# One layer of a streaming encoder on one core: gate writes on another queue, a later exponential, attention values on halves of the array's columns, other banks for the last tiles' branches

## The chip, the cores and the metric

The kernel runs on one core of a Trainium2 chip. The metric is device time in microseconds (us), the median over runs of the whole program. The engines are TensorE (PE, with its weight loads as PEld), VectorE (DVE), ScalarE (ACT), GpSimd (POOL) and SyncE (SP, which in this kernel only issues DMAs). ACT and SP each issue DMAs on a queue of their own, ACTq and SPq in the profile. The clock that TensorE is granted (PEclk) is given as a share of full speed.

## The reference, cut to what matters

One layer on 512 tokens of 1024 channels, all float32. The parts that the change touches are the attention's product with the values, the two branches' output projections, and the choice of 16 experts per head with its softmax.

```python
h = rms_norm(x, attn_norm_g)
q, k, v, qi, ki, wi, glu_in, gates = jnp.split(h @ w_in, _split_points(), axis=-1)
# DSA attention: top-k admissible keys by an indexer score, bias, softmax
probs = jax.nn.softmax(logits, axis=-1).astype(vg.dtype)
y_att = jnp.einsum('bqhk,bqkhd->bqhd', probs, vg) @ w_att_out      # 8 heads of 64
y_conv = conformer_conv(glu_in, conv_w, conv_b, conv_ln_g, conv_ln_b, w_conv_out)
g = jax.nn.sigmoid(gates + b_gate).reshape(B, S, N_BRANCH, D)
x = x + (g[:, :, 0, :] * y_att + g[:, :, 1, :] * y_conv) @ w_out
# PEER mixer on rms_norm(x): 8 heads, 2 x 128 keys, 16 of 256 candidates
sc = jnp.einsum('bshcd,hckd->bshck', q, sub_keys)
sv, si = lax.top_k(sc, PEER_TOPK)
cand_s = (sv[..., 0, :, None] + sv[..., 1, None, :]).reshape(B, S, PEER_HEADS, n_cand)
cand_i = (si[..., 0, :, None] * N_KEYS + si[..., 1, None, :]).reshape(...)
top_s, top_j = lax.top_k(cand_s, PEER_TOPK)
eidx = jnp.take_along_axis(cand_i, top_j, axis=-1)
gate = jax.nn.softmax(top_s.astype(jnp.float32), axis=-1)
act = jax.nn.gelu(jnp.einsum('tnd,td->tn', expert_u[eidx], h)) * gate
x = x + jnp.einsum('tn,tnd->td', act, expert_v[eidx])
# x += sigmoid(rms_norm(x) W_g) * (p W_p)
```

## The kernel before, in words

The 512 tokens are four tiles of 128. Tile 0 goes ahead of tiles 1 to 3. Its experts are gathered row by row (POOL's indirect DMAs, `grow`, with DVE's products `grow` and `acc`); tiles 1 to 3 (384 tokens, TD) go through all 16,384 experts densely, 128 experts at a time. The stages, by the span's clock:

- 0 to about 300 us: the projection `w_in`, the attention of tile 0 and the indexer.
- 300 to 408 us: branches, residual and query of tile 0, with the attention of tiles 1 to 3 mixed in. For each tile and each pair of heads, `softmax` makes the logits (L550), and `weigh` transposes the probabilities (L570, evicted at L572 into `PT`), multiplies `V` by them (L576) and evicts the result (L580). `V`'s 128 columns are those of two heads and `PT` holds the probabilities of both, so each product forms four 64x128 blocks, of which the two on the diagonal are used.
- 408 to 457 us: `branches` for tiles 1 to 3, with 128x384 products in four PSUM banks per half of the channels (`nat_T`, L141). L629 multiplies each by its gate. PSUM has three pools of banks: `mm`, `at` and `tp`.
- 457 to 592 us: residual, per-layer embedding and the query of the mixer.
- 592 to 955 us, the warm stage: 64 steps `u_step`, each of 24 products of 128x384 (L972 to L974) into a `tp` bank, evicted by ACT through Gelu (`sg`, L975). ACT and DVE split each block of expert weights, loaded by SP (`ut`, L961), into `uh` (L964) and `ul` (L965). Mixed into these steps is `gates_dense` for tiles 1, 2 and 3: `select` finds the 16 experts of each head and their gates (`ijg`, written by L711 and L736), PE transposes them (L910), DVE makes one-hot rows (L930 to L933), `scatter` multiplies them (L948, L949), ACT evicts into `stg` (L951), and four DMAs of 512 KB for every 32 tokens write `G_d` in DRAM (L956). There are 12 such bursts of four. `G_d` is read back from 955 us on (`gi`).
- 955 to 1700 us: the other 64 blocks of experts, and the products with `vt`. Then 75 us for what is left of the mixer and for the embedding.

The order of the instructions on each engine is found by a scheduler from the order of the program's text, the buffers and some priorities (`high_priority` for the loads and the split of `ut`); `work()` is advanced in steps between the `u_step`s. The order is fixed when the kernel is built. An engine runs its instructions in that order, and an issue on SP or ACT that has to wait holds up what stands behind it. ACT's Exp and its Gelu use different function tables; each change is an ACT_TABLE_LOAD of 1.28 us.

`select` is a generator in three pieces: the candidates, then the first `lookup` (which of the candidates, as sums over 16 masks on DVE), then the second.

Of the kernel before, what the change touches and what calls it, by code (L numbers as in the profile page):

```python
# [11 lines left out]
F32 = mybir.dt.float32  # L12
# [6 lines left out]
ALU = mybir.AluOpType  # L19
# [5 lines left out]
P = 128  # L25
# [43 lines left out]
def layer_kernel(ctx: ExitStack, tc: tile.TileContext, a, out):  # L69
# [7 lines left out]
    def mm(name="mm"):  # L77
        return psum.tile([P, 512], F32, name="mm", bufs=4)
# [4 lines left out]
    def tp():  # L83
        return psum.tile([P, 512], F32, name="tp", bufs=2)
# [28 lines left out]
    class Stream:  # L113
# [16 lines left out]
            if self.hook:  # L130
                self.hook(n)

        def nat_T(self, pieces, K, x):
            M = sum(p[2] for p in pieces) // P
            ps = [mm()[:, :x.shape[-1]] for _ in range(M)]
            for c0 in range(0, K, 2):
                raw, _ = self.load(pieces, c0)
                self.behind()
                for c in range(2):
                    for m in range(M):  # L140
                        pe.matmul(ps[m], raw[:, c, m * P:(m + 1) * P], x[:, c0 + c, :], start=(c0 + c == 0),  # L141
                                  stop=(c0 + c == K - 1))
            return ps
# [418 lines left out]
    def weigh(ap_, top, qt, pr_, L):  # L562
        nk = qt + 1
        PT = ap_.tile([P, top, 2, P], F32, name="PT", bufs=2)
        for k0 in range(0, nk, 2):
            n = min(2, nk - k0)
            p = tp()
            for kk in range(n):
                for s in range(2):
                    pe.transpose(p[:, (2 * kk + s) * P:(2 * kk + s + 1) * P],  # L570
                                 L[:, s, (k0 + kk) * P:(k0 + kk + 1) * P], ident)
            act.activation(PT[:, k0:k0 + n], p[:, :2 * n * P].rearrange("p (k s q) -> p k s q", k=n, s=2), AF.Copy)  # L572
        yield
        av = tp()[:, :2 * P]
        for kt in range(nk):
            pe.matmul(av, V[:, kt, pr_ * P:(pr_ + 1) * P], PT[:, kt].rearrange("p s q -> p (s q)"),  # L576
                      start=(kt == 0), stop=(kt == nk - 1))
        for s in range(2):
            sl = slice(64 * s, 64 * s + 64)
            act.activation(attT[sl, pr_, qt * P:(qt + 1) * P], av[sl, s * P:(s + 1) * P], AF.Copy)  # L580
        yield

    def attention(ap_, tiles):
# [35 lines left out]
    def branches(pl, q0, N, mixed, mlo=None, tick=None):  # L619
        mix = []  # L620
        for br, (w, x2) in enumerate(((a["w_att_out"], attT), (a["w_conv_out"], convT))):
            for n in range(2):
                ps = W.nat_T([(w, 512 * n, 512)], 4, x2[:, :, q0:q0 + N])
                for m in range(4):
                    c = 4 * n + m
                    g = pl.tile([P, N], F32, name="gld", bufs=4)
                    sp.dma_start(out=g, in_=gT_d[8 * br + c][:, q0:q0 + N])
                    y = pl.tile([P, N], F32, name=f"ymx{br}", bufs=8 - 6 * br)
                    v.scalar_tensor_tensor(y, g, 1.0, ps[m], op0=ALU.add, op1=ALU.mult)  # L629
                    if br == 0:  # L630
                        mix.append(y)
                    elif mlo is None:
                        v.tensor_add(mixed[:, c, :], y, mix[c])
                    else:
                        v.tensor_add(y, y, mix[c])
                        act.activation(mixed[:, c, :], y, AF.Copy)
                        v.tensor_sub(mlo[:, c, :], y, f(mixed[:, c, :]))
                if tick:
                    tick(BTICK)
# [64 lines left out]
    def select(t, gate, i_out, j_out):  # L704
# [17 lines left out]
        for h in range(H):  # L722
# [6 lines left out]
        yield  # L729
        ex = sl_.tile([P, H, 16], F32, name="ex", bufs=1)  # L730
        v.tensor_tensor(out=ex, in0=ts, in1=ts[:, :, 0:1].to_broadcast([P, H, 16]), op=ALU.subtract)
        act.activation(ex, ex, AF.Exp)
        sm = sl_.tile([P, H], F32, name="exs", bufs=1)
        v.tensor_reduce(out=sm, in_=ex, axis=AX, op=ALU.add)
        v.reciprocal(sm, sm)
        v.tensor_tensor(out=gate.rearrange("p (k h) -> p h k", h=H), in0=ex,  # L736
                        in1=sm.unsqueeze(2).to_broadcast([P, H, 16]), op=ALU.mult)
        w = sl_.tile([P, P], F16, name="wpos", bufs=1)
        v.tensor_copy(w.rearrange("p (k h) -> p k h", h=H), tj.rearrange("p h k -> p k h"))
        sT = sl_.tile([P, 2, 16, H], F16, name="sT", bufs=1)  # L740
        v.tensor_copy(sT.rearrange("p c k h -> p h c k"), si[:, t].rearrange("p (h c) k -> p h c k", c=2))
        dl = sl_.tile([P, 3, 16, H], F16, name="dl", bufs=1)
        v.tensor_copy(dl[:, 1], dstart)
        act.activation(dl[:, 0:3:2, 0], sT[:, :, 0], AF.Copy)
        v.tensor_sub(dl[:, 0:3:2, 1:16], sT[:, :, 1:16], sT[:, :, 0:15])
        mk = sl_.tile([P, 16, P], F16, name="mk", bufs=1)
        md = sl_.tile([P, 2, 16, P], F16, name="md", bufs=1)
# [9 lines left out]

        lookup(w, edges[:, 0], 0, 2)
        yield
        add(i_out, md[:, 0, 0], md[:, 0, 1])  # L760
        add(mk[:, 0], md[:, 1, 0], md[:, 1, 1])
        v.tensor_sub(w, w, mk[:, 0])
        lookup(w, edges[:, 1], 2, 1)
        add(j_out, md[:, 0, 0], md[:, 0, 1])
        yield

    def sel0():
# [174 lines left out]
    def scatter(tt, part, t0, q0, stg, ohj, og):  # L942
# [10 lines left out]
        if t0 + q0 == 12:  # L953
            c0 = tt * P + 32 * part
            for b0 in range(0, P // 4, 8):
                act.dma_start(out=G_d[b0:b0 + 8, :, c0:c0 + 32, :].rearrange("b j t f -> j b (t f)"),  # L956
                              in_=stg[:, b0:b0 + 8].rearrange("p b t f -> p b (t f)"))

    def u_prep(i):
# [277 lines left out]
```

## Time and profile before

| | us |
|---|---|
| median of 3 runs | 1781.04 |
| lowest and highest run | 1773.59, 1781.09 |
| the profiled run's own time | 1776.63 |
| span of the profiled run | 1774.9 |
| PE busy in it | 1717.2 (97%) |
| DVE busy | 1362.3 (77%) |
| ACT busy | 660.9 (37%) |

The span is the time from the first to the last instruction in the profile; 1.7 us of the run lie around it. The profiled run took 4.4 us less than the median. A busy share is a mean over the whole span, so a stage that waits is not to be seen in it; the rows further below are taken by stage.

### The profile page before, as it was taken

The numbers are of one execution on the slowest core, as the hardware profiler recorded it, in microseconds if no ns is written. First come the engines' busy times: TensorE is split into PE (matmuls) and PEld (weight loads), VectorE is DVE, ScalarE is ACT, GpSimd is POOL, SyncE is SP. The second block draws the span as 40 slices with busy tenths as digits, with TensorE's granted clock in tenths as the row PEclk, the third lists the DMA queues.
The fourth block names the chain that finished last, engine by engine and source line by source line (L and its number), as shares of the span: only waits on it lengthen the run. The fifth ranks groups of instructions, "written<-read, shape, count | busy, mean of one in ns | idle before, by whom it ended". The sixth has DMA issues, their size and how long they took to land.

```text
span 1774.9 us, 24360 instructions
## 1 busy us (share of the span) xinstructions
PE 1717.2 (97%) x9033; PEld 1487.6 (84%) x9033; DVE 1362.3 (77%) x2489; ACT 660.9 (37%) x981; POOL 427.5 (24%) x301
## 2 busy tenths in 40 slices
PE   6999999999999899999999999999999999999998
PEld 5777677586788888999999999999999988888887
DVE  4889779648769999996857878877877857667763
ACT  3233343340353244444444333333333333334431
POOL 0021000211112113120113645445545511111100
PEclk9999999999999999999999999999999999999999
DMA  5432325756875468788899999899989878888921
GB/s 163 145 120 84 100 84 184 255 174 192 293 266 155 129 227 280 236 273 260 288 293 378 391 329 337 321 340 330 353 306 344 308 260 311 311 291 314 376 87 69
DMA packets 189815, 441.74 MB, mean 249 GB/s; under 512 B 15192, under 2 KB 76888, under 8 KB 189440
## 3 DMA queue, kind: packets, MB, share of 16 engines
q1 hardware_dynamic: 100528, 273.72, 45.1%
q0 software_dynamic: 36864, 134.23, 21.4%
q10 hardware_dynamic: 52304, 32.24, 6.1%
q8 instruction: 71, 1.16, 0.3%
q14 instruction: 48, 0.39, 0.1%
HBM read 391.86 MB, written 52.46 MB: 250 GB/s over the span
## 4 chain that ended last, share of the span: by engine, by line
PE 59%; DVE 7%; issue 4%; DMA 2%; ACT 1%; POOL 0%; SPq 0%; DVEq 0%; ACTq 0%; POOLq 0%
PE tp L972 9%; PE tp L973 9%; PE tp L974 9%; PE mm L1059 6%; PE mm L1060 6%; PE mm L1061 6%; PE at L1060 3%; PE at L1061 3%; PE at L1059 3%; DMA wr<-in_w_ple_gate_dram 1%; PE mm L948 1%; PE mm L949 1%; DVE ul L965 1%; DVE si L702 1%; DVE sc L699 1%
## 5 line engine op out<-in xcount | busy, mean ns | idle before, releaser
L972 PE MATMUL tp<-h_hi,uh 128*128 128x384 f32 x1024 | 350.9, 343 | 11.5 <-ACT sg L975 11.5
L973 PE MATMUL tp<-h_lo,uh 128*128 128x384 f32 x1024 | 347.7, 340 | 0.0
L974 PE MATMUL tp<-h_hi,ul 128*128 128x384 f32 x1024 | 347.4, 339 | 0.0
L799 POOL DMA_INDIRECT grow<-in_peer_u_dram,eidx x128 | 189.0, 1476 | 480.9 <-DVE grow L812 198.2
L799 POOL DMA_INDIRECT grow<-in_peer_v_dram,eidx x128 | 187.3, 1463 | 398.6 <-DVE grow L812 197.9
L1052 DVE TENSOR_TENSOR vl<-vt,vh 128x1024 fp32r<-128x1024 f32 x128 | 156.4, 1222 | 107.7 <-ACT vh L1051 107.5
L964 ACT ACTIVATE uh<-ut 128x1024 fp32r<-128x1024 f32 x128 | 135.5, 1060 | 277.0 <-PE tp L973 252.8
L965 DVE TENSOR_TENSOR ul<-ut,uh 128x1024 fp32r<-128x1024 f32 x128 | 155.8, 1219 | 79.2 <-ACT uh L964 64.4
L972 PEld LDWEIGHTS tp<-h_hi,uh 128*128 128x128 f32 x1024 | 194.7, 190 | 14.6 <-ACT sg L975 13.4
L1051 ACT ACTIVATE vh<-vt 128x1024 fp32r<-128x1024 f32 x128 | 134.9, 1056 | 185.4 <-PE at L1061 138.1
L1059 PE MATMUL mm<-vh,ah 128*128 128x512 f32 x512 | 200.0, 391 | 0.0
L1060 PE MATMUL mm<-vl,ah 128*128 128x512 f32 x512 | 199.2, 389 | 0.3 <-DVE vl L1052 0.3
L1061 PE MATMUL mm<-vh,al 128*128 128x512 f32 x512 | 199.5, 390 | 0.0
L973 PEld LDWEIGHTS tp<-h_lo,uh 128*128 128x128 f32 x1024 | 194.8, 190 | 1.1
L974 PEld LDWEIGHTS tp<-h_hi,ul 128*128 128x128 f32 x1024 | 194.9, 190 | 0.0
L814 DVE SCALAR_TENSOR_TENSOR acc<-grow,gact,acc 128x1024 f32<-128x1024 f32 x128 | 164.3, 1283 | 0.0
L812 DVE SCALAR_TENSOR_TENSOR grow<-grow,h2row 128x1024 f32<-128x1024 f32 x128 | 155.0, 1215 | 5.0 <-DMA grow<-in_peer_u_dram,eidx 5.0
L161 ACT ACTIVATE whi<-wraw 128x1024 fp32r<-128x1024 f32 (+1 forms) x70 | 71.6, 1022 | 178.9 <-PE mm L176 76.5
L162 DVE TENSOR_TENSOR wlo<-wraw,whi 128x1024 fp32r<-128x1024 f32 (+1 forms) x70 | 82.0, 1174 | 42.8 <-ACT whi L161 38.5
L1061 PEld LDWEIGHTS mm<-vh,al 128*128 128x128 f32 x512 | 96.1, 188 | 20.7
L1060 PEld LDWEIGHTS mm<-vl,ah 128*128 128x128 f32 x512 | 96.1, 188 | 19.6 <-DVE vl L1052 0.7
L1059 PEld LDWEIGHTS mm<-vh,ah 128*128 128x128 f32 x512 | 96.1, 188 | 18.8
(310 smaller groups left out, 3191.5 us busy)
## 6 DMA issues: line engine op xcount, KB each, us to landing
ut<-in_uT_dram SPq DMA_DIRECT2D x128, 512.0 KB
vt<-in_peer_v_dram SPq DMA_DIRECT2D x128, 512.0 KB
G_d<-stg ACTq DMA_DIRECT2D x48, 512.0 KB
gi<-G_d SPq DMA_DIRECT2D x32, 768.0 KB
wraw<-in_w_in_dram SPq DMA_DIRECT2D x32, 512.0 KB
wraw<-in_w_peer_q_dram SPq DMA_DIRECT2D x32, 512.0 KB
sg_d<-sg SPq DMA_DIRECT2D x32, 384.0 KB
sgl<-sg_d SPq DMA_DIRECT2D x32, 384.0 KB
```

The lines of the kernel that those rows point to most:

```text
L799: pool.indirect_dma_start(out=r, out_offset=None, in_=a["peer_v" if kind else "peer_u"], in_offset=bass.IndirectOffsetOnAxis(ap=eidx[:, s: ...
L812: v.scalar_tensor_tensor(r, r, 1.0, h2row, op0=ALU.mult, op1=ALU.mult, accum_out=dots[:, s:s + 1])
L814: v.scalar_tensor_tensor(acc, rows.pop(k), gact[:, s:s + 1], acc, op0=ALU.mult, op1=ALU.add)
L964: act.activation(uh, ut, AF.Copy)
L965: anchor[0] = v.tensor_sub(ul, ut, f(uh)).ins
L972: pe.matmul(p, uh[:, c, :], xh, start=(c == 0), stop=False)
L973: pe.matmul(p, uh[:, c, :], xl, start=False, stop=False)
L974: pe.matmul(p, ul[:, c, :], xh, start=False, stop=(c == DC - 1))
L1052: anchor[0] = v.tensor_sub(vl, vt, f(vh)).ins
L1059: pe.matmul(o, xh, vh[:, ks], start=first, stop=False)
L1060: pe.matmul(o, xh, vl[:, ks], start=False, stop=False)
L1061: pe.matmul(o, xl, vh[:, ks], start=False, stop=last)
```

## The change

There are five edits. (a) `nat_T` can be given the pools of its four banks, and `branches` of tiles 1 to 3 gives the second half of the channels two `at` and two `tp` banks in the place of four `mm` banks. (b) `weigh` makes two products of 64 columns for each key tile, each for one head, with outputs on partitions 0 to 63 and 64 to 127 of one bank, and evicts both with one instruction. (c) In `select` the exponential stands behind the first lookup, and its sum, reciprocal and product behind the second. (d) A small copy into `dl` goes from ACT to DVE. (e) The writes of `G_d` go from ACT's queue to SP's.

```diff
-        def nat_T(self, pieces, K, x):
+        def nat_T(self, pieces, K, x, banks=None):
             M = sum(p[2] for p in pieces) // P
-            ps = [mm()[:, :x.shape[-1]] for _ in range(M)]
+            ps = [(banks[m] if banks else mm)()[:, :x.shape[-1]] for m in range(M)]
...
-        av = tp()[:, :2 * P]
+        av = tp()[:, :P]
         for kt in range(nk):
-            pe.matmul(av, V[:, kt, pr_ * P:(pr_ + 1) * P], PT[:, kt].rearrange("p s q -> p (s q)"),
-                      start=(kt == 0), stop=(kt == nk - 1))
-        for s in range(2):
-            sl = slice(64 * s, 64 * s + 64)
-            act.activation(attT[sl, pr_, qt * P:(qt + 1) * P], av[sl, s * P:(s + 1) * P], AF.Copy)
+            for s in range(2):
+                pe.matmul(av[64 * s:64 * s + 64], V[:, kt, pr_ * P + 64 * s:pr_ * P + 64 * s + 64], PT[:, kt, s],
+                          start=(kt == 0), stop=(kt == nk - 1))
+        act.activation(attT[:, pr_, qt * P:(qt + 1) * P], av, AF.Copy)
...
-                ps = W.nat_T([(w, 512 * n, 512)], 4, x2[:, :, q0:q0 + N])
+                ps = W.nat_T([(w, 512 * n, 512)], 4, x2[:, :, q0:q0 + N],
+                             (at, at, tp, tp) if n and mlo is not None else None)
...
-        act.activation(ex, ex, AF.Exp)
-        sm = sl_.tile([P, H], F32, name="exs", bufs=1)
-        v.tensor_reduce(out=sm, in_=ex, axis=AX, op=ALU.add)
-        v.reciprocal(sm, sm)
-        v.tensor_tensor(out=gate.rearrange("p (k h) -> p h k", h=H), in0=ex,
-                        in1=sm.unsqueeze(2).to_broadcast([P, H, 16]), op=ALU.mult)
...
-        act.activation(dl[:, 0:3:2, 0], sT[:, :, 0], AF.Copy)
+        v.tensor_copy(dl[:, 0:3:2, 0], sT[:, :, 0])
...
         lookup(w, edges[:, 0], 0, 2)
         yield
+        act.activation(ex, ex, AF.Exp)
...
         add(j_out, md[:, 0, 0], md[:, 0, 1])
+        sm = sl_.tile([P, H], F32, name="exs", bufs=1)
+        v.tensor_reduce(out=sm, in_=ex, axis=AX, op=ALU.add)
+        v.reciprocal(sm, sm)
+        v.tensor_tensor(out=gate.rearrange("p (k h) -> p h k", h=H), in0=ex,
+                        in1=sm.unsqueeze(2).to_broadcast([P, H, 16]), op=ALU.mult)
...
-                act.dma_start(out=G_d[b0:b0 + 8, :, c0:c0 + 32, :].rearrange("b j t f -> j b (t f)"),
+                sp.dma_start(out=G_d[b0:b0 + 8, :, c0:c0 + 32, :].rearrange("b j t f -> j b (t f)"),
                               in_=stg[:, b0:b0 + 8].rearrange("p b t f -> p b (t f)"))
```

The edits change the fixed order in more places than the diff shows. ACT at the end of the warm stage, in the order of before: the last group of evictions, the four writes of `G_d`, and two steps' evictions behind them.

```order
448 L975 ACTIVATE sg<-tp 128x384
449 L951 ACTIVATE stg<-mm 128x4x32x4 x2
450 L964 ACTIVATE uh<-ut 128x1024
451 L975 ACTIVATE sg<-tp 128x384
452 L951 ACTIVATE stg<-mm 128x4x32x4 x4
453 L956 DMA G_d<-stg 128x8x128 x4
454 L975 ACTIVATE sg<-tp 128x384
455 L964 ACTIVATE uh<-ut 128x1024
456 L975 ACTIVATE sg<-tp 128x384
```

The same place in the order of the changed kernel:

```order
414 L975 ACTIVATE sg<-tp 128x384
415 L951 ACTIVATE stg<-mm 128x4x32x4 x2
416 L964 ACTIVATE uh<-ut 128x1024
417 L975 ACTIVATE sg<-tp 128x384
418 L951 ACTIVATE stg<-mm 128x4x32x4 x2
419 L964 ACTIVATE uh<-ut 128x1024
420 L975 ACTIVATE sg<-tp 128x384
```

The writes are gone from ACT, and each step's `sg` stands directly behind its `uh`. The exponential in tile 3's `select` stood so on ACT:

```order
333 L951 ACTIVATE stg<-mm 128x4x32x4 x2
334 L732 ACT_TABLE_LOAD
335 L732 ACTIVATE ex<-ex 128x128
336 L956 DMA G_d<-stg 128x8x128
337 L964 ACTIVATE uh<-ut 128x1024
338 L956 DMA G_d<-stg 128x8x128 x3
339 L964 ACTIVATE uh<-ut 128x1024
340 L975 ACT_TABLE_LOAD
341 L975 ACTIVATE sg<-tp 128x384
```

In the changed kernel it is line L754, and it stands so:

```order
332 L951 ACTIVATE stg<-mm 128x4x32x4 x2
333 L754 ACT_TABLE_LOAD
334 L754 ACTIVATE ex<-ex 128x128
335 L964 ACTIVATE uh<-ut 128x1024
336 L975 ACT_TABLE_LOAD
337 L975 ACTIVATE sg<-tp 128x384
```

One `uh` is left between the two table loads, where there were two and four writes. SP in the last third of the warm stage, in the order of the changed kernel:

```order
176 L956 DMA G_d<-stg 128x8x128 x3
177 L961 DMA ut<-in_uT_dram 128x1024
178 L956 DMA G_d<-stg 128x8x128
179 L1002 DMA sg_d<-sg 128x768
180 L961 DMA ut<-in_uT_dram 128x1024 x2
181 L1002 DMA sg_d<-sg 128x768
182 L961 DMA ut<-in_uT_dram 128x1024 x2
183 L956 DMA G_d<-stg 128x8x128 x4
184 L1002 DMA sg_d<-sg 128x768
185 L961 DMA ut<-in_uT_dram 128x1024 x2
```

In before, SP has only the `ut` and `sg_d` rows here; now a burst of `G_d` stands between two loads of `ut`, whole or three and one. PE at the second part of tile 2's transposes (`ijg`, L910) in before:

```order
2799 L949 LDWEIGHTS ohj
2800 L949 MATMUL mm<-og,ohj 128x128
2801 L910 MATMUL mm<-ident,ijg 128x128 x2
2802 L948 LDWEIGHTS ohj
2803 L948 MATMUL mm<-og,ohj 128x128
```

And in the changed kernel:

```order
2878 L949 MATMUL mm<-og,ohj 128x128
2879 L972 MATMUL tp<-h_hi,uh 128x384
2880 L973 MATMUL tp<-h_lo,uh 128x384
...
2888 L972 MATMUL tp<-h_hi,uh 128x384
2889 L973 MATMUL tp<-h_lo,uh 128x384
2890 L910 MATMUL mm<-ident,ijg 128x128 x2
2891 L974 MATMUL tp<-h_hi,ul 128x384
```

In before they follow 25 whole steps; in the changed kernel they stand behind 26 steps, all of tile 1's `scatter` and 11 products of the step after it. On DVE, between the start of the stage and the row that makes `ijg` ready for them (L711), two more `ul` and one more `acc` stand in the changed kernel.

## Rows read from the trace of the kernel before

**Rows 1.** The page, section 1: busy time of each engine, share of the span, instructions.

```profile
PE 1717.2 (97%) x9033; PEld 1487.6 (84%) x9033; DVE 1362.3 (77%) x2489; ACT 660.9 (37%) x981; POOL 427.5 (24%) x301
```

**Rows 2.** Windows: length; busy PE, PEld, DVE, ACT, POOL (instructions); PEclk; DMA share; GB/s.

```profile
408.00:457.00 49.00, 45.98 (x147) 26.45 (x146) 40.77 (x158) 6.89 (x12) 3.04 (x3) 1.00 0.68 219
...
592.00:645.00 53.00, 47.15 (x261) 46.03 (x261) 52.97 (x229) 18.87 (x27) 9.21 (x7) 0.97 0.64 198
645.00:726.00 81.00, 75.36 (x572) 71.60 (x570) 79.82 (x156) 38.46 (x64) 22.00 (x7) 0.98 0.80 255
726.00:955.00 229.00, 225.17 (x1612) 219.65 (x1613) 171.10 (x224) 103.12 (x166) 31.16 (x24) 0.98 0.87 281
955.00:1700.00 745.00, 745.00 (x3611) 657.76 (x3611) 573.65 (x617) 273.67 (x317) 287.29 (x200) 1.00 0.90 325
```

**Rows 3.** PE's waits, windows 408:457, 592:645, 645:726, 726:955: total, times, longest.

```profile
PE mm L141 <- DVE ymx L629: 2.9, 3, 1.3
...
PE tp L972 <- ACT sg L975: 5.9, 2, 2.9
...
PE tp L972 <- ACT sg L975: 1.9, 2, 1.7
PE mm L948 <- ACT stg L951: 1.7, 2, 1.5
...
PE tp L972 <- ACT sg L975: 3.7, 2, 1.9
```

**Rows 4.** Timeline of DVE around `ijg`: start, duration, instruction.

```profile
644.33 0.28 DVE L711 TENSOR_TENSOR ijg<-md 128x128 f32<-128x128 f16 x1
...
725.75 0.28 DVE L711 TENSOR_TENSOR ijg<-md 128x128 f32<-128x128 f16 x1
...
726.13 1.22 DVE L965 TENSOR_TENSOR ul<-ut,uh 128x1024 fp32r<-128x1024 f32 x1
```

**Rows 5.** Timeline of PE in the warm stage; in brackets the idle time before and its releaser.

```profile
644.67 0.44 PE L910 MATMUL mm<-ident,ijg 128*128 128x128 f32 x2
...
726.09 0.67 PE L910 MATMUL mm<-ident,ijg 128*128 128x128 f32 x2 [2.06 <-DVE ijg L711]
...
735.16 0.34 PE L974 MATMUL tp<-h_hi,ul 128*128 128x384 f32 x1
...
937.37 0.45 PE L972 MATMUL tp<-h_hi,uh 128*128 128x384 f32 x1 [1.87 <-ACT sg L975]
```

**Rows 6.** Windows behind two of PE's waits (columns as in rows 2).

```profile
770.50:774.00 3.50, 3.50 (x12) 3.50 (x12) 3.50 (x5) 2.11 (x5) 0.00 (x0) 0.51 0.83 259
...
938.00:942.00 4.00, 4.00 (x17) 4.00 (x16) 3.51 (x4) 1.59 (x3) 1.08 (x1) 0.60 0.89 224
```

**Rows 7.** Timeline of ACT in the warm stage.

```profile
821.56 1.06 ACT L964 ACTIVATE uh<-ut 128x1024 fp32r<-128x1024 f32 x1 [2.06 <-PE tp L973]
...
928.57 8.20 ACTq L956 DMA_DIRECT2D G_d<-stg  x4
```

**Rows 8.** Timeline of PE around one pair's `weigh` (L576) and `softmax` (L550).

```profile
363.01 1.46 PE L576 MATMUL tp<-PT,V 128*128 128x256 f32 x6
364.31 1.95 PE L141 MATMUL mm<-h,wraw 128*128 128x128 f32 x16
366.19 1.13 PE L550 MATMUL at<-k_T,q_T 64*128 64x512 f32 x4
367.25 0.60 PE L141 MATMUL mm<-h,wraw 128*128 128x128 f32 x3
```

**Rows 9.** All instructions of L576: count, duration ns min/median/max, first and last start.

```profile
L576 PE MATMUL tp<-PT,V x80: 377/379/483, 223.7 to 401.9; 128*128 128x256 f32 x80
```

**Rows 10.** DMA queues, 805 to 830 us: packets, MB, share of 16 engines' time.

```profile
q1 hardware_dynamic: 1119, 3.73, 44.5%
q10 hardware_dynamic: 4160, 2.10, 27.8%
```

**Rows 11.** Timeline of SP: first issue's start, time to the last issue's end.

```profile
808.44 5.49 SPq L961 DMA_DIRECT2D ut<-in_uT_dram  x2
```

## The prediction

> **What bounds the kernel now.** I read the page's busy times first: PE is busy 97% of the span [rows 1], so a gain must come from the 58 us in which it is not, from PE's own work, or from its clock. The windows by stage say where those 58 us are. From 955 to 1700 us PE is busy in all of 745.0 us, and nothing in the change touches that stage. From 408 to 457 it lacks 3.0 us, from 592 to 645 5.9, from 645 to 726 5.6, from 726 to 955 3.8 [rows 2]. But from 592 to 726 DVE is busy in 132.8 of 134 us [rows 2], so there PE's gaps are mostly the shadow of DVE. After 726 DVE has air (171 of 229 us) and PE's stalls count in full.
>
> The waits of PE then say for whom it stops in these stages: three times for L629 on DVE (2.9 us), and in the warm stage nearly always for `sg`, Gelu's eviction on ACT: 5.9, 1.9 and 3.7 us, with 1.7 us for `stg` [rows 3]. ACT is 37% busy [rows 1], so it isn't short of time; the timeline shows it held up. Four issues of `G_d` stand on it from 928.57 for 8.20 us [rows 7], and PE's next step waits 1.87 us for the `sg` behind them, at 937.37 [rows 5]. Near 770 us it is a table load for Gelu behind the exponential and two `uh`, as the order of ACT shows.
>
> Each such wait is paid twice. In the windows behind two of them the granted clock is 0.51 and 0.60 [rows 6]: most of 3.5 and 4 us at the lower of the two levels, 1.2 in place of 2.4 GHz, after PE had stood still. That costs (1-0.51)x3.5 = 1.7 and (1-0.60)x4 = 1.6 us.
>
> **The change part by part**, against the profiled run's 1776.6 us.
>
> *(a) Banks of the branches.* The three waits for L629 are PE waiting for a bank of `mm` that the gates' products have not read out. With other banks for the second half the first group of each branch's half needn't wait: at most 2.9 us [rows 3]. The rest of the stage keeps its DVE work (40.8 of 49 us [rows 2]), so the wait should not come back. Bounds 0 and -2.9; I take -2.5.
>
> *(b) `weigh`.* L576 has 80 records of 256 columns [rows 9]. Six of them start at 363.01 and the next instruction at 364.31 [rows 8]: 0.217 us each, 17.3 us in all. The change streams 64 weight columns for each head, so 160 records of 128 columns. If the halves go one after the other, they cost the same 17.3 us; if they go side by side, half, 8.7 us less. The trace has no product on halves of columns; the nearest is L550, on halves of the rows: four passes of 512 columns in 1.06 us (366.19 to 367.25 [rows 8]). One after the other they would take 4x2x0.217 = 1.73 us, side by side 0.87, so they do run side by side, with 0.19 us on top. Before them, 16 records of 128 columns take 1.88 us, by the same pace 16x0.108 = 1.73; 0.15 more. So a change into halves and out again costs 0.35 to 0.4 us. There are 16 visits (4 tiles, 4 pairs): 16x0.4 = 6.4 us, some of it shared where `weigh` stands beside L550. Net -8.7+6.4 = -2.3 us. Bounds: -8.7 with no cost of the change of form, +6.4 with the halves in series. I take -2.3, as L550 does. The 16 evictions fewer on ACT are worth nothing, since nothing waits for ACT's time there.
>
> The Trainium skill, in "TensorEngine Tiling (Array Packing)", section Key Properties, says that a change of the tiling mode drains TensorE, and that different tiles can multiply in parallel. The first speaks against this edit, the second for it; the 0.35 us about L550 agree with both, and only the sum of the two decides. Taken without the drain it would be -8.7 us.
>
> *(c), (d) The exponential later, the copy to DVE.* They keep ACT from standing still behind DVE. Up to 645 that buys nothing: the 5.9 us of waits lie at 621 and 629 us, but PE's next need of DVE is `ijg`, ready at 644.61 with PE's transposes at 644.67 [rows 4, 5]. DVE does the same work before it, plus a small copy. So 0, with +0.5 as a bound. Cover: the saturated DVE.
>
> For tile 2 the same need comes at 726.09, with a wait of 2.06 us and then the lower clock [rows 5]. In the changed order the second transposes stand 11 products into the 27th step. In before PE reaches that place at 735.16 [rows 5]. DVE, which has `ijg` ready at 726.03 now, has two more `ul` and one more `acc` before it, three operations of 1,024 columns; at 1.22 us each [rows 4] it comes to 726.03+3.7 = 729.7, and a little sooner, since a few small rows of the selection go behind. So PE can gain 735.2-729.7 = 5.5 us by there, hardly more; what it has to lose is more than that (5.6 us without work from 645 to 726 [rows 2], and clock behind it). If it waits for `ijg` again, the clock may fall again, 1.7 us. Bounds -3.8 and -6.7; I take -5.
>
> At 770 us one `uh` is left between the two table loads on ACT where two and four issues stood. The 1.9 us (half of the 3.7 of [rows 3]) and the 1.7 us of clock behind [rows 6] should go: -3.6, bounds 0 and -3.6, for the table loads themselves stay.
>
> *(e) `G_d` on SP.* At 937 the same sum: 1.87+1.6 = -3.5 us. The 1.7 us for `stg` and 1.9 for `sg` of 645 to 726 are within the cap above. In the rest of the stage ACT's issues cost PE nothing now. What is late next is what stands behind the bursts on SP: loads of `ut` and the writes of `sg_d`. A load issued at 808.44 [rows 11] is split at 821.56 [rows 7], so it can come 13.1 us after its issue. One load has 3.73 MB/7.1 = 0.52 MB, and takes 0.445x25/7.1 = 1.6 us of all engines; a burst takes 0.278x25 = 7.0 us [rows 10]. Behind a whole burst that is 8.6 us if nothing else moves; it fits. I put +1.5 us for a stall or two, bounds 0 and +34 (rival 3).
>
> The Trainium skill's "DMA: Bandwidth & Descriptors", section Issuing engines are not separate DMA queues, holds that issuing from several engines only saves the sequencer's time. By it this edit moves the sequencers' time alone, 8.20 us a burst, from ACT to SP; the trace agrees in so far as `G_d` and `ut` share the same 16 engines [rows 10].
>
> *Sum:* -2.5-2.3+0-5-3.6-3.5+1.5 = -15.4, so 1761.2 us on the profiled run's scale. That run is 0.25% below the median, 1781.04; from the median it is 1765.6. I say **1763 us**, between the two.
>
> **The rivals.**
>
> 1. *The halves go in series.* Everything else as above, but (b) is +6.4 in place of -2.3: 1763+8.7 = 1772. For it: no record of column halves in the trace. Against it: L550's halves [rows 8]. It would also hold if each product's weight load (now twice as many) stands in the way.
>
> 2. *DVE takes back the warm stage.* If DVE's order keeps PE waiting for `ijg` or `ul` as now, 645 to 735 gives 0 in place of -5, and only 770, 937 and the stages before 592 remain: 1763+5 = 1768. For it: 132.8 of 134 us [rows 2]. Against it: the cap above is reached with DVE's work as it is.
>
> 3. *Slower: the loads behind the bursts come late.* On one queue, `ut` stands behind 2 MB of `G_d`. If a burst gets only what the loads' queue leaves (44.5% is taken [rows 10]), it takes 7.0/0.555 = 12.6 us, and the load behind it lands 14.2 us after its issue, past the 13.1 that it has. That is 1.1 us late and 1.7 of clock, 2.8 us for each of 12 bursts, 34 us: 1763-1.5+34 = 1795. The point from which it decides is a landing 13 us after the issue. Against it: the order splits most bursts with a `ut` between, and the loads that compete are mostly those of the same queue.
>
> The Trainium skill has the ground for this rival: in "DMA: Bandwidth & Descriptors", section Queues, rings and completion order, under HWDGE ordering, SP and ACT each own one ring on every engine, consumed in ring order. No row here shows a `ut` behind a burst.
>
> 4. *No effect:* the stalls move and return as others, all but (a): 1763+13 = 1776.
>
> **How the numbers follow.** The forecast 0.52, halves in series 0.13, DVE 0.15, loads late 0.09, no effect 0.11. The range: 1749 has (b) at its lower bound of -8.7 (6.4 less) and then no stall on SP (1.5), and 6 for the upper bounds of the other terms and the 4.4 us between the two scales (1763-6.4-1.5-6 = 1749); 1778 is 2 us above no effect, and takes in all but the slower case. A difference of 0.5%, about 9 us, is what a measurement of this kernel can tell from none. Faster by more than that (below 1772): the forecast, DVE's case, and half of the series case, less their tails, 0.66. Within 0.5%: no effect, the other half of the series case, and the tails, 0.24. Slower: 0.10.
>
> **What would show it.** (a) no wait for L629 in 408 to 457, or one under 0.5 us. (b) L577's records in pairs that start together, 16 visits of 0.5 to 1.0 us, and 360 to 408 shorter by 2 us. (c), (d) `ijg` for tile 1 at about 640 (644.6 less what (a) and (b) give, 4.8), for tile 2 at about 725 (729.7 less the same), and PE there no more than 2 us before it. No wait for `sg` over 1 us at 770 or 937, and a clock of 1.00 behind. (e) no wait of ACT behind an issue; `ut`'s issues on SP a little later, and DVE's and ACT's rows of `uh` and `ul` with no new wait for a DMA. The prediction is wrong if PE waits for `uh` or `ul` behind a DMA, if L577 costs 17 us or more, or if PE's transposes for tile 2 come past 728.

## The result, and the profile after

| | before | after |
|---|---|---|
| median of 8 runs each | 1777.13 us | 1766.16 us |
| lowest and highest run | 1773.59, 1781.09 | 1760.41, 1775.34 |
| the profiled run | 1776.63 us, clock 0.992 | 1775.34 us, clock 0.988 |

The ratio is 0.9937, with a 95% interval of 0.9919 to 0.9954: 11 us less (1777.13-1766.16). The forecast was 14 to 18 us less on its two scales, with a range of 1749 to 1778. One run of exp_free, an experiment below, took 4883 us and is left out of its ratio.

A reader who lays the two profiles side by side sees only 1.3 us. The profiled run of after is the slowest of its eight, at the lowest clock: the eight go from 1760.41 us at a mean clock of 0.995 to 1775.34 at 0.988, and 0.007 of 1770 us is 12 of those 15 us. So here stages are compared between two places of the program that both kernels pass, not between two times of the clock. The windows of after (columns as in [rows 2]), which answer to the first four of [rows 2]:

```profile
408.00:457.00 49.00, 47.90 (x175) 29.82 (x174) 39.24 (x157) 6.14 (x13) 3.26 (x3) 1.00 0.66 217
...
592.00:645.00 53.00, 46.39 (x256) 45.52 (x255) 49.56 (x211) 17.96 (x25) 9.53 (x9) 0.94 0.64 191
645.00:726.00 81.00, 78.71 (x599) 75.28 (x598) 80.90 (x159) 40.88 (x66) 29.19 (x8) 0.99 0.84 266
726.00:955.00 229.00, 225.31 (x1623) 219.46 (x1621) 178.44 (x247) 106.48 (x170) 40.72 (x25) 0.98 0.88 287
```

PE gained where it was wanted: from 645 to 726 us it lacks 2.3 us of work, where it lacked 5.6, and DVE is busy in 80.9 of the 81. From 592 to 645 it lacks more (6.6 for 5.9) at a lower clock. PE's waits in the same four windows, which answer to [rows 3]:

```profile
PE mm L190 <- DVE wlo L162: 0.8, 1, 0.8
...
PE tp L972 <- ACT sg L975: 5.7, 1, 5.7
...
PE mm L910 <- DVE mk L711: 2.2, 1, 2.2
...
PE tp L972 <- ACT sg L975: 3.5, 1, 3.5
```

The three waits for L629 are gone, and so are those for `stg` and those for `sg` from 645 to 942. Two waits for `sg` are left, each longer than any in before. The clock behind the places where before stalled, and behind the new stall (the first two rows answer to [rows 6]):

```profile
770.50:774.00 3.50, 3.50 (x33) 3.34 (x32) 3.50 (x4) 1.88 (x4) 1.88 (x1) 1.00 1.01 348
938.00:942.00 4.00, 4.00 (x25) 4.00 (x24) 0.00 (x0) 0.00 (x0) 0.00 (x0) 1.00 1.02 416
947.00:951.00 4.00, 3.63 (x11) 3.63 (x12) 3.74 (x4) 3.11 (x5) 0.00 (x0) 0.50 0.96 379
```

At 770 and 938 the clock is 1.00 where it was 0.51 and 0.60; but from 947 to 951 it is 0.50. The timeline of PE says what stands ahead of that, and at tile 2's and tile 1's transposes:

```profile
649.33 0.44 PE L910 MATMUL mm<-ident,ijg 128*128 128x128 f32 x2
...
724.49 0.45 PE L910 MATMUL mm<-ident,ijg 128*128 128x128 f32 x1 [2.23 <-DVE mk L711]
...
734.08 0.44 PE L910 MATMUL mm<-ident,ijg 128*128 128x128 f32 x2
...
947.37 0.69 PE L972 MATMUL tp<-h_hi,uh 128*128 128x384 f32 x1 [3.45 <-ACT sg L975]
```

The wait of 1.87 us at 937 [rows 5] is gone, and one of 3.45 us stands ahead of 947. Four views of after show its chain. SP issues the last burst and then the read-back `gi`; the DMA view of 924 to 944 us gives `gi`'s time to landing (the last number); DVE and ACT wait for it.

```profile
924.51 6.85 SPq L956 DMA_DIRECT2D G_d<-stg  x4
...
934.42 1.17 SPq L1020 DMA_DIRECT2D gi<-G_d  x2
```

```profile
gi<-G_d SPq DMA_DIRECT2D x2, 768.0 KB, 10.9
```

```profile
944.04 0.96 DVE L1038 TENSOR_TENSOR sg<-sg,gi 128x768 f32<-128x768 f32 x1 [6.26 <-DMA gi<-G_d]
```

```profile
945.08 0.89 ACT L1042 ACTIVATE ah<-sg 128x768 fp32r<-128x768 f32 x1 [8.15 <-issue]
945.87 1.05 ACT L964 ACTIVATE uh<-ut 128x1024 fp32r<-128x1024 f32 x1
946.82 0.51 ACT L975 ACTIVATE sg<-tp 128x384 f32<-128x384 f32 x1
```

ACT has stood for 8.15 us in front of `ah`, the first expert weights times gates, which needs `gi`; PE's `sg` stands two instructions behind. In the order of before three `sg` stood between the issues and `ah`. The read-back is there too, and sooner than the 955 us given in the stages of the kernel before. These are SP's issue and DVE's first use of it in before:

```profile
939.90 0.80 SPq L1020 DMA_DIRECT2D gi<-G_d  x2
...
945.22 0.96 DVE L1038 TENSOR_TENSOR sg<-sg,gi 128x768 f32<-128x768 f32 x1 [3.43 <-DMA gi<-G_d]
```

From the issue to the use it takes 5.3 us in before and 9.6 in after (934.42 to 944.04).

Lengths of stages in us, from PE's timeline in one profile of each kernel (the kernels but the first two are experiments, below). One profile says little about a few us: the seven kernels that have both (a) and (b) take 285.0 to 290.7 us in the first row. The ends are: the first L141; the first `u_step`; tile 1's second transposes; the 33rd and the 41st `u_step`; the last `scatter` product; the first product with `vh`; the span's end.

| stage | before | after | only_writes | only_select | no_select |
|---|---|---|---|---|---|
| first L141 to first `u_step` | 289.8 | 289.8 | 289.4 | 290.5 | 288.2 |
| to tile 1's transposes | 55.0 | 55.6 | 55.2 | 55.8 | 55.2 |
| to the 33rd step | 118.4 | 113.4 | 111.5 | 115.2 | 111.5 |
| to the 41st | 43.9 | 40.2 | 40.2 | 40.2 | 40.2 |
| to the last `scatter` | 119.9 | 119.9 | 119.9 | 120.9 | 119.9 |
| to the first `vh` | 28.8 | 31.3 | 29.4 | 27.5 | 26.7 |
| to the end | 819.2 | 819.4 | 818.7 | 818.8 | 818.8 |

After gains 5.0+3.7 = 8.7 us in two stages, and gives back 0.6+2.5 in two others. It also starts the first row 4.1 us late (303.94 against 299.88 us). The windows of the stretch before it have a lower clock in after:

```profile
195.00:210.00 15.00, 13.15 (x58) 10.37 (x59) 5.79 (x11) 5.93 (x9) 1.01 (x1) 0.73 0.27 95
210.00:225.00 15.00, 15.00 (x57) 11.12 (x55) 10.86 (x29) 5.84 (x13) 0.85 (x1) 0.81 0.37 99
```

In before the two have 0.80 and 0.98.

The 2.5 us at the first `vh` are those of this one profile. In the seven profiles of kernels with the writes on SP and `ah` on ACT the stage takes 26.7 to 31.3 us, 29.0 in the mean; in the five with the writes on ACT 27.5 to 29.3, 28.7 in the mean. So over all of them what the wait at 937 cost is not gained, and not much is lost either.

### The profile page after: what moved, and what is told of

The parts are those of the page before. It is cut to its first block, busy times and chain, and to the rows that moved or that the text cites. A ratio compares the mean times of both kernels' runs of the same rounds, so it can differ in the third digit from the quotient of the medians.

```text
span 1773.6 us, 24517 instructions
## 1 busy us (share of the span) xinstructions
PE 1714.6 (97%) x9113; PEld 1483.7 (84%) x9113; DVE 1361.8 (77%) x2493; ACT 655.4 (37%) x961; POOL 438.9 (25%) x301
## 4 chain that ended last, share of the span: by engine, by line
PE 55%; DMA 2%; DVE 2%; issue 1%; ACT 1%; SPq 0%; DVEq 0%; ACTq 0%
PE tp L972 8%; PE tp L973 8%; PE tp L974 8%; PE mm L1059 6%; PE mm L1061 6%; PE mm L1060 6%; PE at L1059 3%; PE at L1061 3%; PE at L1060 3%; DMA wr<-in_w_ple_gate_dram 1%; PE mm L948 1%; PE mm L949 1%; PE mm L1112 1%; PE mm L1114 1%; PE mm L1113 1%
## 5 line engine op out<-in xcount | busy, mean ns | idle before, releaser
L799 POOL DMA_INDIRECT grow<-in_peer_u_dram,eidx x128 | 199.4, 1558 | 476.6 <-DVE grow L812 197.6
```

What stands on the lines that cost most here:

```text
L799: pool.indirect_dma_start(out=r, out_offset=None, in_=a["peer_v" if kind else "peer_u"], in_offset=bass.IndirectOffsetOnAxis(ap=eidx[:, s: ...
```

## The experiments

Twelve kernels, each with its times beside runs of before on the same chip.

**Each edit alone.** The four kernels are before plus one edit of the change, (c) and (d) together.

only_banks:

```diff
-                ps = W.nat_T([(w, 512 * n, 512)], 4, x2[:, :, q0:q0 + N])
+                ps = W.nat_T([(w, 512 * n, 512)], 4, x2[:, :, q0:q0 + N],
+                             (at, at, tp, tp) if n and mlo is not None else None)
```

> Edit (a) alone on the kernel before. By the prediction's step: no wait for L629 between 408 and 457 us, and 2.5 us off the end. Rival, from the trace after the change: the stage of the branches gets about 3.9 us shorter, and the next one, the residual, as much longer, because PE then waits for the split weights (wlo, L162); the first u_step starts where it did and the time is the same within 1 us.

Ratio 0.9998 (0.9985 to 1.0012): no change. The rival holds. The stage of the branches in its windows, and PE's waits from 453 to 592 us:

```profile
408.00:457.00 49.00, 49.00 (x166) 30.64 (x165) 42.28 (x161) 7.66 (x14) 3.26 (x3) 1.00 0.69 233
```

```profile
PE mm L177 <- DVE wlo L162: 4.5, 5, 2.3
...
PE mm L190 <- DVE wlo L162: 1.3, 1, 1.3
PE mm L662 <- DVE wlo L162: 0.6, 1, 0.6
```

In before PE's waits for `wlo` from 457 to 592 us are these alone:

```profile
PE mm L177 <- DVE wlo L162: 5.2, 6, 1.3
```

PE is busy in all 49.0 us, 3.0 more than in before, and then waits longer for the split weights of the residual (`wlo`), 6.4 us for 5.2. In the changed kernel the last 128x384 product of the branches comes at 453.45 us and the first at 412.49, 41.0 us apart for 44.8 in before; the first `u_step` follows it by 140.3 us for 136.4. In that profile what the banks give is given back to 0.1 us; in only_banks itself the two lengths are 41.0 and 139.1. Over all profiles, the nine kernels with the other banks have 41.0 and 140.0 us in the mean, the five without 44.9 and 137.0: of 3.9 us, 3.0 are given back. The waits for `wlo` show 1.2 us of it in only_banks; the rest I take from the lengths.

only_weigh:

```diff
+            for s in range(2):
+                pe.matmul(av[64 * s:64 * s + 64], V[:, kt, pr_ * P + 64 * s:pr_ * P + 64 * s + 64], PT[:, kt, s],
```

> Edit (b) alone. By the prediction's step: visits of 0.5 to 1.0 us, 2.3 us off the end. Rival 1, halves in series: 6 us more. From the trace after the change I now expect pairs that run side by side, some 5 us less of PE's time, and at the end between 0 and 5 us less, depending on what PE waits for next between 300 and 410 us.

Ratio 1.0004 (0.9990 to 1.0019): no change. But PE's timeline shows that the products do what they are meant to. A visit for a third tile:

```profile
359.52 0.88 PE L577 MATMUL tp<-PT,V 128*64 128x128 f32 x12 [0.35 <-ACT PT L572]
360.32 2.05 PE L141 MATMUL mm<-h,wraw 128*128 128x128 f32 x16
362.31 1.13 PE L550 MATMUL at<-k_T,q_T 64*128 64x512 f32 x4
```

Twelve records take 0.80 us, 0.067 each, where one alone would take 0.108: they run side by side. A visit of tile 0 and one of the last tile have 4 and 16 records:

```profile
221.63 0.44 PE L577 MATMUL tp<-PT,V 128*64 128x128 f32 x4
222.00 0.49 PE L550 MATMUL at<-k_T,q_T 64*128 64x128 f32 x2
...
395.18 1.09 PE L577 MATMUL tp<-PT,V 128*64 128x128 f32 x16
396.21 1.05 PE L141 MATMUL mm<-h,wraw 128*128 128x128 f32 x7
```

So 4, 12 and 16 records take 0.37, 0.80 and 1.03 us: each further record 0.055, half of 0.108, and about 0.15 us once in a visit. The 16 records behind the visit at 359.52 take 1.99 us for 1.88 in [rows 8], so the way back costs 0.1. Against the 1.30 us of [rows 8] that visit saves 0.4 us. The stage from the first L141 to the branches' first 128x384 product takes 104.5 us for 108.5 (in the profile of after, at a lower clock, it is 108.6).

Where does that go? Some of it goes into waits in the same stage. PE's two waits there that are longer than in before, first before (300 to 408 us), then only_weigh (300 to 411):

```profile
PE mm L141 <- DMA wraw<-in_w_conv_out_dram: 0.9, 1, 0.9
```

```profile
PE mm L141 <- DMA wraw<-in_w_conv_out_dram: 2.2, 2, 1.6
PE tp L210 <- DVE amx L554: 1.1, 1, 1.1
```

All of PE's waits from the first L141 to the branches come to 4.5 us in before, 6.2 in only_weigh and 8.4 in after; the five profiles with the old product have 4.4 to 5.3, the eight with the halves (weigh_twice, below, aside) 5.8 to 10.2. The other part is in the run's mean clock: 0.990 over its 12 runs, against 0.9917 over the 30 of before beside them (single runs scatter by about 0.002, so a mean of 12 by 0.0005). 0.0017 of 1777 us is 3.0 us. As an estimate, if each run's time is reduced by what its clock cost, (1-clock) times its span, this kernel has 1759.9 and before 1763.1: 3.2 us less, against 3.0 us of clock. That the edit is what brings the clock down is not shown by this.

only_select:

```diff
-        act.activation(dl[:, 0:3:2, 0], sT[:, :, 0], AF.Copy)
+        v.tensor_copy(dl[:, 0:3:2, 0], sT[:, :, 0])
...
+        act.activation(ex, ex, AF.Exp)
         add(i_out, md[:, 0, 0], md[:, 0, 1])
```

> Edits (c) and (d) alone; the G_d writes stay on ACT. By the prediction's step: nothing up to tile 1's transposes, the wait for sg near 770 us gone (about 3.6 us less at the end), 937 us as before. Rival: ACT stands behind the exponential instead of the copy, PE waits once for longer near 625 us, and the end is the same within 1 us.

Ratio 0.9977 (0.9964 to 0.9991), 4 us less. The prediction's step holds: tile 1's transposes 55.8 us behind the first step, no gain, and 3.6 us less between the 33rd and the 41st. There is one longer wait in the place of two, 5.7 us up to 628.63, as the rival had it, which doesn't touch the rest. 3.2 us more are gained before the 33rd step, and 1.0 is lost behind the 41st: there two of the `G_d` issues hold ACT for 6.40 us, and PE waits 0.79 us for `sg`, at 811.19.

only_writes:

```diff
-                act.dma_start(out=G_d[b0:b0 + 8, :, c0:c0 + 32, :].rearrange("b j t f -> j b (t f)"),
+                sp.dma_start(out=G_d[b0:b0 + 8, :, c0:c0 + 32, :].rearrange("b j t f -> j b (t f)"),
```

> Edit (e) alone. By the prediction's step: no wait for sg behind an issue at 675, 770 and 937 us, tile 2's transposes of ijg later in PE's order; 6 to 9 us less at the end. Rival: the loads and the first read-back of G_d come later behind the bursts on SP, PE waits near 943 us behind the first ah, and 2 to 4 us of it are given back, so 4 to 6 us less. Slower rival of the prediction: waits for uh or ul behind a load, over 10 us more.

Ratio 0.9959 (0.9944 to 0.9974), 7 us less. PE's waits from 645 to 726, and from 726 to 960:

```profile
PE mm L910 <- DVE mk L711: 2.4, 1, 2.4
```

```profile
PE tp L972 <- ACT sg L975: 2.5, 1, 2.5
```

From 645 to 940 us all waits for ACT are gone; one for DVE stays at tile 2's transposes, and the new one for `sg` stands at the handover. So the step holds in size, and the first rival in its place: 6.9+3.7 us gained, and the 3.5 us that 937 should have given are spent on the new wait. PE waits for no `uh` or `ul` between 645 and 940, in this kernel or in after. The DMA view of after from 645 to 940 us gives the loads' median time from issue to landing as the last number:

```profile
ut<-in_uT_dram SPq DMA_DIRECT2D x57, 512.0 KB, 5.3
```

The load that comes closest is issued at 700.11, lands 8.2 us later and is split at 709.40, 1.1 us after that. The slower rival does not come about.

This edit also changes the fixed order on ACT. Near 770 us before has two `uh` between the two table loads, at 762.22 and, after 4.09 us of waiting for PE, at 767.37; only_writes has one (773.60), as only_select has. No run here has the writes on SP in the order of before, so how much of the 7 us is the issues' time on ACT, and how much the new order, stays open.

**Edits undone from the changed kernel.** no_weigh and no_select are the changed kernel without edit (b), and without (c) and (d):

```diff
-            for s in range(2):
-                pe.matmul(av[64 * s:64 * s + 64], V[:, kt, pr_ * P + 64 * s:pr_ * P + 64 * s + 64], PT[:, kt, s],
```

> The changed kernel with the old product with the values (all but edit b). The theory now is that the halves save about 4 us of PE's time between 300 and 410 us, and that the clock takes it back: the runs of edit (b) alone show a mean granted clock of 0.990, those of before 0.992. Then this kernel should run at a higher mean clock than the changed one, by about 0.002, and take the same time within 2 us. Rival, that the halves pay as the prediction's step had it: 2 to 4 us slower than the changed kernel, at the same clock.

Ratio 0.9950 (0.9934 to 0.9967), a median of 1767.58 us, with a mean clock of 0.9932 against 0.9925 in the changed kernel. By the ratios it is 2.3 us slower than the changed kernel (0.9937), which is the rival's size and not the expected one; but the intervals overlap, and a difference of 0.0007 in the clock is within its scatter from run to run. The three kernels timed with it that have the halves and the writes on SP (no_select, first_block, exp_ready) have medians of 1764.2 to 1764.9 us, some 3 us less, but they differ in other edits too. So it stays open whether the halves pay in the changed kernel.

```diff
-        v.tensor_copy(dl[:, 0:3:2, 0], sT[:, :, 0])
+        act.activation(dl[:, 0:3:2, 0], sT[:, :, 0], AF.Copy)
...
-        act.activation(ex, ex, AF.Exp)
         add(i_out, md[:, 0, 0], md[:, 0, 1])
```

> The changed kernel with the old place of the exponential and the copy on ACT (all but edits c and d). If the gains add up, as the two single edits' ratios (0.9977 and 0.9959) suggest, it lies 4 us above the changed kernel, at 0.996 of before. Rival, from the traces of the single edits: both remove the same wait near 770 us, so together they give no more than the writes alone, and this kernel is as fast as the changed one within 1.5 us, at 0.994.

Ratio 0.9937 (0.9919 to 0.9955), as the changed kernel. The gains don't add up; the table above shows why. Between the 33rd and the 41st step, 3.7 us go with either edit, and with both no more. With the writes on SP, (c) and (d) bring nothing that the times show.

**The handover at 943 us.** first_block writes first what is read back first:

```diff
-            for b0 in range(0, P // 4, 8):
+            for b0 in (16, 24, 0, 8):
```

> The changed kernel, with the four writes of a burst in another order: the block of rows that is read back first (16 to 23) is written first, and rows 0 to 15 last. If PE's wait of 3.45 us near 943.6 us comes from the read-back gi standing behind the whole last burst, gi is issued up to 5 us sooner and the wait shrinks: 2 to 5 us less. Rival, that the read-back is slow because of the loads beside it (10.9 us from issue to landing): the wait and the time stay within 1 us.

Ratio 0.9933 (0.9915 to 0.9951). PE's wait there is 1.6 us in its profile, for 3.5; but no_select, with the old order of the writes, has 1.4. One profile each does not show that the order did it, and the time, within 1 us of the changed kernel, is the rival's. The edit also did little of what it was for: `gi` is issued 8.4 us behind the burst's first issue, for 9.9 in after and 8.9 in no_select, and lands 10.6 us later, for 10.9.

first_on_dve takes the first `ah` off ACT:

```diff
-        act.activation(ah, sgv, AF.Copy)
+        if m:
+            act.activation(ah, sgv, AF.Copy)
+        else:
+            v.tensor_copy(ah, sgv)
```

> The changed kernel, with the first copy into ah on DVE and not on ACT, so that ACT isn't held by the read-back gi between two steps' sg. If that is what PE waits for near 943.6 us (3.45 us and the lower clock behind it), the time from the last scatter product to the first product with vh falls from 31.3 to about 26.5 us, and the whole by 2 to 5 us. Rival: PE then waits as long for ul, which stands behind the same read-back on DVE, or for vt, and the time stays.

PE's waits from 726 to 960 us:

```profile
PE mm L1063 <- DVE vl L1055: 0.8, 1, 0.8
PE mm L1062 <- ACT vh L1054: 0.7, 1, 0.7
PE mm L948 <- DVE og L933: 0.2, 1, 0.2
```

The wait for `sg` is gone, and the last `scatter` product is followed by the first `vh` after 25.9 us for 31.3, so ACT's place in front of `ah` was what held PE. The length alone would not show it, since no_select has 26.7 with `ah` on ACT; both_first has 26.4. But the ratio is 0.9944 (0.9926 to 0.9963): PE now comes sooner to products whose splits (`vh`, `vl`) aren't there, and ACT waits 6.8 us for `vt` from 936 to 965 us. Of the 12.7 us by which this profile is ahead of before at the first `vh`, 11.0 are left at the last.

both_first has the two edits above.

> first_block and first_on_dve together on the changed kernel, as the version that might beat both: if the read-back and ACT's place are the two halves of the stall at the end of the warm stage, 4 to 6 us less than the changed kernel, about 0.990 to 0.991 of before. Rival: no more than first_block alone, 0.993.

Ratio 0.9929 (0.9903 to 0.9955), a median of 1763.43 us. It is the lowest median of all, but the interval holds the changed kernel's ratio; that it beats it is not shown, and the rival holds.

**Is the wait at 627 us hidden?** exp_ready and exp_free take the exponential of scores that lie ready and leave out the subtraction before it, so their gates are other numbers; exp_free has four buffers for the result.

```diff
-        ex = sl_.tile([P, H, 16], F32, name="ex", bufs=1)
+        ex = sl_.tile([P, H, 16], F32, name="ex", bufs=4)
...
-        act.activation(ex, ex, AF.Exp)
+        act.activation(ex, s0, AF.Exp)
```

> The changed kernel, with the exponential taken of the first keys' scores, which lie ready, and not of the chosen candidates' differences, so that ACT never waits for DVE there (the gates are other numbers, and one small subtraction on DVE is left out). If PE's wait of 5.7 us near 627 us is hidden behind DVE, as the prediction's step has it, that wait goes, PE waits for ijg instead, and the time is the same as that of the changed kernel within 2 us. Rival: it comes off in full, with the clock behind it, 6 to 8 us less.

Ratio 0.9927 (0.9910 to 0.9945). It didn't take the wait away: with one buffer the exponential stood behind the tile before, and PE waited 4.7 us for `sg`, up to 624.40. Hence the next.

> As exp_ready (the exponential of the first keys' scores, so the gates are other numbers), with four buffers for its result, since with one buffer it waited for the gates' product of the tile before. Now nothing holds ACT between 605 and 640 us. If DVE hides PE's wait near 627 us, tile 1's transposes of ijg come 55 us after the first u_step as they do in the changed kernel and before (55.6 and 55.0), and the time is that of exp_ready within 2 us. Rival: they come 5 us sooner, and the time falls by 5 to 8 us.

Ratio 0.9952 (0.9936 to 0.9969). That is 4.4 us more than exp_ready by the ratios, where 2 were expected; the intervals overlap, and the times don't decide. Now ACT is free, and PE's timeline has:

```profile
634.71 0.34 PE L971 MATMUL tp<-h_hi,uh 128*128 128x384 f32 x1
639.67 0.48 PE L909 MATMUL mm<-ident,ijg 128*128 128x128 f32 x1 [4.62 <-DVE ijg L711]
```

The wait for ACT became one for DVE, 4.6 us; tile 1's second transposes come 56.9 us behind the first step, for 55.6 in after. So the long wait is hidden behind DVE, as the prediction had it.

**Does edit (b)'s time go to the clock?** weigh_twice is edit (b) alone, with its sums made twice:

```diff
-        for kt in range(nk):
+        for kt in 2 * list(range(nk)):
             for s in range(2):
```

> Edit (b) alone, with each sum over the key tiles made twice, the second in place of the first, so that PE is as busy in weigh as before, on halves. It tells why the runs of edit (b) alone show a mean clock of 0.990 against 0.992. If the clock falls because PE gets ahead and then waits, the clock here is that of before, 0.992, and the time that of before within 2 us. If the products on halves themselves bring it down, the clock is 0.990 or lower, and the time 3 to 6 us longer.

Ratio 1.0033 (1.0014 to 1.0051), a mean clock of 0.9909 over 12 runs. Neither came out: the time is 6 us longer, at a clock between the two. Its stage up to the branches is 112.9 us long for 108.5, so it costs more than the products of before and is not the equal of them that it was meant to be. Whether being ahead or the halves themselves bring the clock down stays open.

## Why the prediction was right, and where its steps were not

The sign, the size within a third, and the place (the warm stage) came out; the sum was -15.4 us, and the measured one is -11. That the number came so close is in part luck: two terms gave nothing that is shown, one was spent again, and two that came out in size stood under edits that aren't needed for them.

- **(a) -2.5 us: wrong, 0.** The step said that the wait should not come back, because DVE had air in that stage. It did not look at what PE does next: the residual's weights were not ready enough sooner, and the stage behind took back 3.0 of the 3.9 us gained. The cost of the wait was right, its price at the end was not.
- **(b) -2.3 us: right in mechanism, mis-sized, and not shown in time.** The halves run side by side. The prediction put a change of form and back at 0.35 to 0.4 us, from L550; it measures 0.15 in the visit and 0.1 behind it. With 16x0.26 = 4.2 in place of 6.4 us the same sum gives -4.5 of PE's time. It left out that PE then waits: 1.7 us more in the same stage in only_weigh, 3.9 in after. Alone the edit changes nothing in time (1.0004), at a lower mean clock, 0.990 for 0.9917; in the changed kernel it stays open. The Trainium skill's "TensorEngine Tiling (Array Packing)", section Key Properties, has both: the drain at a change of mode, which agrees with the 0.15 and 0.1 us, and tiles that work in parallel, which agrees with 0.055 us a record for 0.108.
- **(c), (d) up to tile 1's transposes 0: right.** 55.0 us became 55.6, although PE's wait for `sg` there is 5.7 us; exp_free shows DVE right behind it.
- **Tile 2's transposes -5: right in size, under the wrong edit.** From the first step to the place that [rows 5] has at 735.16, before takes 145.5 us and after (734.28, behind the transposes at 734.08) 140.5: 5.0 less. DVE sets the end, but one step sooner than I put it: PE waits 2.2 us at the first transposes, at 724.49, and none at the second. It stands under (c) and (d), but the writes alone bring 7.5 us to that place (138.0), and (c) and (d) alone 2.4 (143.1). The upper bound of -6.7 has no working. The prediction's own sign of being wrong, these transposes past 728 us, did appear: they come at 734.08 for about 725. 4.1 us of that are the late start of that profile, and 4.8 are what (a) and (b) were to give by then.
- **770 us, -3.6: right in size (43.9 to 40.2), but with two causes.** I gave it to the exponential; the writes alone take it as well, so (c) and (d) are worth nothing beside (e).
- **937 us, -3.5: failed.** The wait went, and one at the handover took its place: `gi` behind the last burst and `ah` in front of `sg` on ACT, 2.5 us more in after's profile and 0.2 in the mean of seven. The prediction named loads of `ut` and writes of `sg_d` as what would be late next, and missed the third transfer behind the bursts, the read-back.
- **SP, +1.5: 0** for the loads: PE waits for no `uh` or `ul` between 645 and 940 us, and the loads land a median 5.3 us after their issue. The 13.1 us that a load was said to have are one load's; another in before is issued at 711.16 and split at 718.81, 7.6 us later. So the condition of rival 3 did not arise. The Trainium skill's "DMA: Bandwidth & Descriptors", section Issuing engines are not separate DMA queues, says that issuing from several engines saves only the sequencers' time. The trace agrees: the issues' time went from ACT (8.20 us for the last burst) to SP (6.85).

By the single edits the writes carry most of the gain, 7 us of 11: 0.9959 alone and 0.9937 with the rest. The intervals overlap, and no run shows which edit the other 4 us belong to, if they are there: (c) and (d) can be undone without loss, (a) gives nothing alone, and for (b) it is open.

## What to carry to other kernels

A wait that disappears is worth only what the next resource allows: follow the program to the next place where the engines meet, and compare the time between two such places in both kernels. Before moving DMAs to another queue, list every transfer that stands behind them, the read-back of the same data first of all, and see what the engine that waits for it has queued behind. Two fixes for one stall don't add up.

## What the runs showed that I had not expected

The spread between runs of one kernel is mostly the clock: 0.995 to 0.988 for 1760 to 1775 us. Reduced by its clock, each of the eight runs of after lies near 1754 us, with a standard deviation of 1.6 us. Edit (b) alone took some 4 us off PE's visits; longer waits in the same stage took back 1.7 of them in its profile, and the lower clock of its runs would account for the rest. Why that clock is lower is open.

A weight load of 64 columns takes less than one of 128: 137 ns for L577, 190 for L576, in the medians of all their instructions.
